# Forming the low half of unscaled weights by an accumulating DMA instead of a VectorE subtraction

## The chip, the cores and the metric

The kernel runs on one core of one Trainium2 chip. Its time is the device time of one execution, in microseconds. Engines are called TensorE (PE, and PEld for its weight loads), VectorE (DVE), ScalarE (ACT), GpSimd (POOL) and SyncE (SP, which issues most DMA transfers).

## The reference, cut to what matters

One layer of a hybrid decoder trunk on x of 1024 tokens by 1024 channels, in float32:

```python
shift, scale, gate = jnp.split(silu(c) @ ada_w + ada_b, 3, axis=-1)
h = rms_norm(x, norm_g) * (1 + scale) + shift
parts = jnp.split(h @ w_in, offsets, axis=-1)     # 16 column groups, 10264 columns
y_sb  = stick_breaking_attention(...) * silu(sz)  # 4 heads of 128
y_gdn = rms_norm(gated_delta_rule(...)) * silu(dz)
y_gla = rms_norm(gla_chunked(...)) * silu(lz)
g_sb, g_gdn, g_gla = jnp.split(sigmoid(mg + merge_b), 3, axis=-1)
merged = g_sb * (y_sb @ proj_sb) + g_gdn * (y_gdn @ proj_gdn) + g_gla * (y_gla @ proj_gla)
return x + gate * (merged @ w_out)
```

Most of the arithmetic is in the dense products: h with the columns of w_in, the three projections and w_out.

## The kernel before, in words

Everything is held transposed, channels on the 128 partitions. A dense product is made from two parts of each operand: the high part is the operand rounded to the fast float32r format, the low part is what the rounding left. Three passes of matmuls (high by high, low by high, high by low) go into one PSUM bank. `split` (L149 to L156) makes the two parts of a weight: ScalarE casts the raw tile into the high part (L151), VectorE subtracts the high part from the raw tile and writes the low part (L152). Where a row scale belongs to the weights, L154 and L155 do the same with the scale.

`load_half` (L161) brings four blocks of 128 rows by 128 columns, 256 KB, into a raw tile by a DMA on SyncE's queue (L163) and splits them. There are three raw tiles and three slots for finished weights (`w`, with both parts of up to eight blocks). `load_w` (L170) makes one slot from one or two halves, for a group of 128 output channels that `run_cm` (L187) works off with 24 matmuls per half of the tokens for eight blocks, or 12 for four. `load_tm` (L176) fills two slots, whi and wlo, for the products with tokens on the partitions; it calls `load_half` too.

`load_w` without a scale serves 56 groups of w_in (the delta rule's heads 1 to 3, the linear attention's q, k and two z for each of four heads, the attention's z, 24 merge gates), proj_sb (eight groups with four blocks) and w_out (eight groups). proj_gla and proj_gdn have scales. The four column groups of the first head of the delta rule advance together in a loop at the start, which calls `split` itself (L345).

Only TensorE's order is written by hand. A planner in the program (`emit`, L247) interleaves the tasks of the three mixers with the dense groups: each task yields estimated waits, and the dense groups fill the time between. `dense` (L234) asks for the weights of a group one group ahead. The order of the instructions on all other engines and on SyncE's queue is made by the framework's scheduler from its own estimates; each engine then runs its list in that order.

The stages: start, norm and the first head (0 to 84 us), the gates' inputs and the first conv (84 to 134 us), the gated delta rule beside dense groups (134 to 500 us), gated linear attention (to 860 us), stick-breaking attention (to 1181 us), merge and output (to 1522 us). In the delta rule each of eight half heads passes a list of small steps: `gdn_prep` (L500; a power on GpSimd in `rstd_cols`, L284; a round trip through DRAM, L555 to L560; 15 pairs of small VectorE steps, L570 and L572; xd out and in, L579 and L594), `gdn_inv` (L582; GpSimd's L596, L602, L628, L631), `gdn_vq` (L680; GpSimd's L720) and `gdn_scan` (L728). The gates' inputs pass GpSimd at L452 and L453, then ScalarE, a scan on VectorE (L473) and transposes on TensorE whose results VectorE copies at L489 and L490.

Of the kernel before, what the change touches and what calls it, by code (L numbers as in the profile page):

```python
# [12 lines left out]
F32 = mybir.dt.float32  # L13
F32R = mybir.dt.float32r
BF16 = mybir.dt.bfloat16
AF = mybir.ActivationFunctionType
ALU = mybir.AluOpType
AX = mybir.AxisListType

P = 128  # L20
# [32 lines left out]
def kernel(ctx: ExitStack, tc: tile.TileContext, xT: bass.AP, c: bass.AP,  # L53
# [3 lines left out]
    nc = tc.nc  # L57
# [15 lines left out]
    def big(tag, w=1024, dt=F32):  # L73
        return mp.tile([P, w], dt, tag=tag, name=tag, bufs=3 if tag == "u5" else 2)

    def mid(tag, w=512, dt=F32):
        return sp.tile([P, w], dt, tag=tag, name=tag, bufs=1 if tag in ONE_MID else 3 if tag in ("c0", "c8", "c9") else 2)
# [67 lines left out]
        mm(ps, ones[0:1, :], crow[0:1, sl], 858, start=True, stop=True)  # L145
        nc.scalar.activation(out=c_row[:, sl], in_=ps, func=AF.Silu)

# [1 line left out]
    def split(hi, lo, raw, scale=None):  # L149
        if scale is None:  # L150
            nc.scalar.copy(out=hi, in_=raw)  # L151
            nc.vector.tensor_sub(out=lo, in0=raw, in1=hi.bitcast(F32))  # L152
        else:
            nc.scalar.activation(out=hi, in_=raw, func=AF.Copy, scale=scale)  # L154
            nc.vector.scalar_tensor_tensor(out=lo, in0=raw, scalar=scale, in1=hi.bitcast(F32),  # L155
                                           op0=ALU.mult, op1=ALU.subtract)  # L156

    def raw_tile():
        return wp.tile([P, 4, P], F32, tag="raw", name="raw")

    def load_half(hi, lo, src, k0, scales=None):  # L161
        raw = raw_tile()
        nc.sync.dma_start(out=raw, in_=src[k0 * P:(k0 + 4) * P, :].rearrange("(k p) n -> p k n", p=P))  # L163
        if scales is None:
            split(hi, lo, raw)
        else:
            for k in range(4):
                split(hi[:, k, :], lo[:, k, :], raw[:, k, :], scales[k])

    def load_w(src, kt=KT, scales=None):  # L170
        w = wp.tile([P, 2, KT, P], F32R, tag="w", name="w")
        for k0 in range(0, kt, 4):
            load_half(w[:, 0, k0:k0 + 4, :], w[:, 1, k0:k0 + 4, :], src, k0, scales)
        return w

    def load_tm(offs):  # L176
        whi = wp.tile([P, KT, 2 * P], F32R, tag="w", name="whi")
        wlo = wp.tile([P, KT, 2 * P], F32R, tag="w", name="wlo")
        for i, o in enumerate(offs):
            cs = slice(i * P, (i + 1) * P)  # L180
            for k0 in (0, 4):
                load_half(whi[:, k0:k0 + 4, cs], wlo[:, k0:k0 + 4, cs], w_in[:, o:o + P], k0)
        return whi, wlo
# [38 lines left out]
            evac(t2, ps)  # L222
            yield

    # a dense group: (load, run); loads are issued one group ahead
    def cm_in(o, evac):
        return (lambda: load_w(w_in[:, o:o + P])), (lambda w: run_cm(w, evac()))

# [60 lines left out]
    def colb(ap, n, w):  # L289
        return ap.unsqueeze(2).broadcast_to([P, n, w])  # L290

# [1 line left out]
    mod = cp.tile([P, 24], F32, name="mod")  # L293

    def conditioning(j, t_w="u6", t_p="u3"):
# [27 lines left out]
    for hf in range(2):  # L323
        nc.scalar.activation(out=rstd[:, hf * HALF:(hf + 1) * HALF], in_=ms[hf], func=AF.Ln,
                             scale=1.0 / D, bias=eps_c)
    nc.scalar.activation(out=rstd, in_=rstd, func=AF.Exp, scale=-0.5)
    amp = cp.tile([P, KT], F32, name="amp")

    # the first head's four column groups advance together as h arrives
    first = (O_DQ, O_DK, O_DV, O_DZ)  # L330
    f_ps = [[None, None] for _ in first]
    f_banks = ((pa, "acc"), (pa, "acc"), (pm, "mx"), (pm, "mx"), (pt, "tr"), (pl, "lv"),
# [1 line left out]
    for k in range(KT):  # L334
        conditioning(k)
        conditioning(8 + k)
        raw = raw_tile()
        wsrc = w_in[k * P:(k + 1) * P, O_DQ:O_DQ + 4 * 512].rearrange("p (g n) -> p g n", g=4)
        nc.sync.dma_start(out=raw, in_=wsrc[:, :, 0:P])
        w = wp.tile([P, 2, 4, P], F32R, tag="w", name="w")  # L340
# [7 lines left out]
        hi = hp.tile([P, T], F32R, tag="h", name="h_hi")  # L348
        lo = hp.tile([P, T], F32R, tag="h", name="h_lo")
# [26 lines left out]
                    mm(f_ps[g][hf], w[:, a, g, :], r[:, sl], 216,  # L376
                       start=(k == 0 and n == 0), stop=(k == KT - 1 and n == 2))

# [1 line left out]
    def conv_silu(r, i, h):  # L380
        t = big(f"u{1 + i}")
        j = 4 * (4 * i + h)
        nc.vector.tensor_scalar(out=t, in0=r[:, 0:T], scalar1=C("conv", j), scalar2=None,
                                op0=ALU.mult)
        for tap in range(1, 4):
            nc.vector.scalar_tensor_tensor(out=t, in0=r[:, tap:tap + T],  # L386
                                           scalar=C("conv", j + tap), in1=t,
                                           op0=ALU.mult, op1=ALU.add)
        return t
# [35 lines left out]
        for hf in range(2):  # L425
            f(hf, slice(hf * HALF, (hf + 1) * HALF), f_ps[i][hf])

# [1 line left out]
    small_w = wp.tile([P, 2, KT, P], F32R, tag="w", name="w")  # L429
    nc.gpsimd.memset(small_w.rearrange("p a k n -> p (a k n)").bitcast(F32), 0.0)  # L430
    raw = big("u7").rearrange("p (k n) -> p k n", k=KT)
    for o, dst, n in ((O_LR, 0, RANK), (O_DB, 32, NH), (O_DA, 64, NH)):
        nc.sync.dma_start(out=raw[:, :, dst:dst + n],
                          in_=w_in[:, o:o + n].rearrange("(k p) n -> p k n", p=P))
# [5 lines left out]
    parts = [mid("v2", dt=F32R)[0:RANK, :] for _ in range(2)]  # L440
# [55 lines left out]
    g_dram = {e: dp.tile([P, T], F32, name=f"g_dram{e[0]}_{e[1]}") for e in EARLY}  # L496
    y_dram = [dp.tile([P, T], F32, name=f"y_dram{i}") for i in range(16)]

# [1 line left out]
    def gdn_prep(st, q):  # L500
        h = st["h"]
        hs = slice(q * HALF, (q + 1) * HALF)
# [290 lines left out]
                                    in0=o[:, i * width:(i + 1) * width],  # L793
                                    scalar1=rs[:, i:i + 1], scalar2=None, op0=ALU.mult)

# [1 line left out]
    def gla_groups(st):  # L797
        h = st["h"]

# [219 lines left out]
                                     in1=st["z"][e_][:, t0:t0 + 256])  # L1019
                nc.sync.dma_start(out=y_dram[8 + 2 * h + e_][:, t0:t0 + 256], in_=y)  # L1020

# [1 line left out]
    sb_v = {}  # L1023

    def sb_groups(st):
# [125 lines left out]
                nc.sync.dma_start(out=y_dram[h][:, sl], in_=y)  # L1151
            yield 1200

# [1 line left out]
    merged = []  # L1155
    gate_t = {}
    ys = {}
# [114 lines left out]
                    gs.append(gate(gi, d + 2))  # L1272
        return gs + [(out_group(d), []) for d in range(KT)]

# [1 line left out]
    L = [{"h": h, "z": []} for h in range(NH)]  # L1276
    SB = [{"h": h} for h in range(NH)]

# [105 lines left out]
```

## Time and profile before

| | |
|---|---|
| median of 3 runs | 1523.69 us (1520.3 to 1524.83) |
| profiled execution | span 1522.0 us, first to last instruction; no other time is shown for it |
| TensorE busy | 1463.0 us, 96% |
| weight loads (PEld) | 1227.5 us, 81% |
| VectorE busy | 861.8 us, 57% |
| ScalarE busy | 676.8 us, 44% |
| GpSimd busy | 175.8 us, 12% |
| DMA | 126.48 MB, mean 83 GB/s; SyncE's queue 27.9% of 16 engines |
| chain of waits | PE 81%, DVE 9%, ACT 4%, POOL 2%, issue 2%, DMA 2% |

A busy time is the sum of an engine's instructions; instructions that only issue a DMA or wait are not in it. The chain of waits is followed back from the last instruction: each piece is what released the next one. An arrow `<-` in a group reads "written from".

### The profile page before, as it was taken

Reading aid. Unit: us, or ns where it says so; the run is one execution under the profiler, and the core shown is the slowest. Engines: PE = TensorE matmul, PEld = TensorE weight load, DVE = VectorE, ACT = ScalarE, POOL = GpSimd, SP = SyncE. Lnnn points to the kernel's source line nnn. Section 1 sums busy time; section 2 is a strip of 40 time slices with the busy share of each in tenths; the row PEclk is TensorE's granted clock in tenths of the full one; section 3 lists DMA queues with packets and bytes.
Section 4 is the critical chain, followed back from the end, with each engine's and each line's share of the span. In section 5 each row is a group of like instructions: output and inputs, shape, how many; then the busy total and the mean of one; then the engine's idle time right before and its main releaser. Section 6 shows DMA issues by size and latency. Waiting matters only on the chain.

```text
span 1522.0 us, 26560 instructions
## 1 busy us (share of the span) xinstructions
PE 1463.0 (96%) x10564; PEld 1227.5 (81%) x10564; DVE 861.8 (57%) x1855; ACT 676.8 (44%) x1473; POOL 175.8 (12%) x306
## 2 busy tenths in 40 slices
PE   4898999999999999999999999999999999999998
PEld 1677787777778887978888999889988888888887
DVE  5978736557653666667666525563555226474621
ACT  4255845462652846556475524342444442322200
POOL 4231222223330000000000100000000000000000
PEclk8899999999999999999999999999999999999999
DMA  6644322131231211212121212111122334353342
GB/s 211 189 119 120 99 87 74 44 88 47 79 93 50 56 43 53 53 32 60 50 67 38 69 49 63 49 36 42 43 69 85 110 104 138 115 149 111 120 143 76
DMA packets 162470, 126.48 MB, mean 83 GB/s; under 512 B 23429, under 2 KB 139269, under 8 KB 162346
## 3 DMA queue, kind: packets, MB, share of 16 engines
q1 hardware_dynamic: 162202, 124.47, 27.9%
q8 instruction: 83, 1.36, 0.4%
q14 instruction: 41, 0.34, 0.1%
q10 hardware_dynamic: 144, 0.31, 0.1%
HBM read 99.80 MB, written 24.95 MB: 82 GB/s over the span
## 4 chain that ended last, share of the span: by engine, by line
PE 81%; DVE 9%; ACT 4%; POOL 2%; issue 2%; DMA 2%; SPq 0%; POOLq 0%; DVEq 0%; ACTq 0%
PE acc L95 66%; PE lv L95 6%; PE mx L95 6%; PE tr L122 3%; DVE u L299 1%; DVE w L152 1%; POOL c L284 1%; DVE u L386 1%; POOL u L453 1%; DVE w L570 1%; DVE w L572 1%; DVE u L1110 1%; DMA u<-in_adaT 1%; POOL w L596 0%; DMA w<-xd 0%
## 5 line engine op out<-in xcount | busy, mean ns | idle before, releaser
L95 PE MATMUL acc<-h_hi,w 128*128 128x512 f32 x1856 | 658.1, 409 | 12.4 <-ACT h_hi L151 5.7
L95 PEld LDWEIGHTS acc<-h_hi,w 128*128 128x128 f32 x1856 | 352.5, 190 | 84.5 <-ACT h_hi L151 6.1
L95 PE MATMUL acc<-h_lo,w 128*128 128x512 f32 x928 | 365.9, 394 | 8.1 <-DVE h_lo L358 7.7
L95 PEld LDWEIGHTS acc<-h_lo,w 128*128 128x128 f32 x928 | 176.9, 191 | 36.9 <-DVE h_lo L358 8.9
L95 PE MATMUL acc<-whi,h_hi 128*128 128x256 f32 x640 | 186.8, 292 | 0.0
L95 PE MATMUL acc<-whi,h_lo 128*128 128x256 f32 x640 | 180.7, 282 | 0.0
L95 PE MATMUL acc<-wlo,h_hi 128*128 128x256 f32 x640 | 180.7, 282 | 0.0
L95 PE MATMUL acc<-u,w 128*128 128x512 f32 x768 | 176.5, 391 | 0.0
L95 PEld LDWEIGHTS acc<-u,w 128*128 128x128 f32 x768 | 144.2, 188 | 31.6
L151 ACT CAST w<-raw 128x512 fp32r<-128x512 f32 x143 | 84.2, 619 | 121.8 <-PE acc L95 90.4
L152 DVE TENSOR_TENSOR w<-raw,w 128x512 fp32r<-128x512 f32 x143 | 98.5, 701 | 50.7 <-ACT w L151 49.9
L95 PEld LDWEIGHTS acc<-whi,h_hi 128*128 128x128 f32 x640 | 122.3, 191 | 1.4 <-issue 0.7
L95 PEld LDWEIGHTS acc<-wlo,h_hi 128*128 128x128 f32 x640 | 122.4, 191 | 0.1
L95 PEld LDWEIGHTS acc<-whi,h_lo 128*128 128x128 f32 x640 | 122.1, 191 | 0.0
L284 POOL TENSOR_TENSOR c<-c,mhalf 128x4 f32<-128x4 f32 (+1 forms) x56 | 54.7, 976 | 578.8 <-DVE c L282 577.4
L95 PE MATMUL acc<-m_hi,w 128*128 128x512 f32 x256 | 79.0, 389 | 0.0
L1110 DVE TENSOR_TENSOR_SCAN u<-u,zero_c 128x128 f32<-128x128 f32 (+7 forms) x32 | 43.4, 1356 | 36.1 <-ACT u L1108 36.1
L155 DVE SCALAR_TENSOR_TENSOR w<-raw,col,w 128x128 fp32r<-128x128 f32 x96 | 29.5, 349 | 55.3 <-ACT w L154 55.3
L95 PEld LDWEIGHTS mx<-r,u 128*128 128x128 f32 x288 | 44.1, 190 | 18.0 <-DVE r L751 4.9
L95 PEld LDWEIGHTS acc<-m_hi,w 128*128 128x128 f32 x256 | 48.0, 188 | 10.0
L95 PE MATMUL mx<-r,u 128*128 128x128 f32 x288 | 48.5, 281 | 6.3 <-POOL u L720 2.7
L95 PE MATMUL lv<-u,u 128*32 128x32 f32 (+5 forms) x528 | 49.2, 252 | 4.1 <-DVE u L653 4.1
(254 smaller groups left out, 2177.6 us busy)
## 6 DMA issues: line engine op xcount, KB each, us to landing
raw<-in_w_in SPq DMA_DIRECT2D x160, 256.0 KB, 3.0
u<-in_adaT SPq DMA_DIRECT2D x24, 512.0 KB, 3.5
g_dram<-v SPq DMA_DIRECT2D x36, 256.0 KB, 2.1
v<-g_dram SPq DMA_DIRECT2D x36, 256.0 KB, 2.6
u<-in_xT SPq DMA_DIRECT2D x16, 512.0 KB, 5.6
u<-y_dram SPq DMA_DIRECT2D x16, 512.0 KB, 3.8
v<-gam_d SPq DMA_DIRECT2D x16, 256.0 KB, 3.5
y_dram<-v SPq DMA_DIRECT2D x16, 256.0 KB, 2.0
```

The costliest lines, as they stand in the source:

```text
L95: return nc.tensor.matmul(out, lhsT=lhsT, rhs=rhs, **kw)
L122: nc.tensor.transpose(out=out, in_=in_, identity=ident[:k, :k])
L151: nc.scalar.copy(out=hi, in_=raw)
L152: nc.vector.tensor_sub(out=lo, in0=raw, in1=hi.bitcast(F32))
L155: nc.vector.scalar_tensor_tensor(out=lo, in0=raw, scalar=scale, in1=hi.bitcast(F32), op0=ALU.mult, op1=ALU.subtract)
L284: nc.gpsimd.tensor_tensor(out=out, in0=out, in1=mhalf[:, 0:n], op=ALU.pow)
L299: nc.vector.tensor_tensor_reduce(out=junk, in0=aw, in1=c_row, scale=1.0, scalar=0.0, op0=ALU.mult, op1=ALU.add, accum_out=mod[:, j:j + 1])
L386: nc.vector.scalar_tensor_tensor(out=t, in0=r[:, tap:tap + T], scalar=C("conv", j + tap), in1=t, op0=ALU.mult, op1=ALU.add)
L453: nc.gpsimd.tensor_scalar(out=gt[0][DA, sl], in0=raw[DA, :], scalar1=C("dt_bias")[DA, :], scalar2=None, op0=ALU.add)
L570: nc.vector.tensor_tensor(out=t3, in0=L3[:, w:16, j:w].broadcast_to([32, n, w]), in1=Xl3[:, j:w, 0:w].broadcast_to([32, n, w]), op=ALU.mult)
L572: nc.vector.tensor_sub(out=Xl3[:, w:16, 0:w], in0=Xl3[:, w:16, 0:w], in1=t3)
L1110: nc.vector.tensor_tensor_scan(om[:, 0:n][:, ::-1], om[:, 0:n][:, ::-1], zero_c.broadcast_to([P, n]), 1.0, ALU.mult, ALU.add)
```

## The change

`load_half` gets a flag that only `load_w` sets. For an unscaled load whose source and destination both have 128 columns, ScalarE casts the raw tile into the high part as before, then writes the negated high part into the low part's place with a second activation, and GpSimd issues a DMA that adds the raw tile (SBUF) onto it (SBUF), each partition's 512 elements as one run. `split` is as it was and still serves the scaled weights, `load_tm`, the first head's loop and all activations. The rest of the diff removes or empties comment lines.

```diff
-    def load_half(hi, lo, src, k0, scales=None):
+    def load_half(hi, lo, src, k0, scales=None, by_dma=False):
         raw = raw_tile()
         nc.sync.dma_start(out=raw, in_=src[k0 * P:(k0 + 4) * P, :].rearrange("(k p) n -> p k n", p=P))
-        if scales is None:
+        if scales is None and hi.shape[-1] == P and src.shape[-1] == P and by_dma:
+            def flat(t):
+                return t.rearrange("p k n -> p (k n)")
+
+            nc.scalar.copy(out=hi, in_=raw)
+            nc.scalar.activation(out=lo, in_=hi.bitcast(F32), func=AF.Copy, scale=-1.0)
+            nc.gpsimd.dma_start(out=flat(lo), in_=flat(raw), accum_op=ALU.add)
+        elif scales is None:
             split(hi, lo, raw)
         else:
             for k in range(4):
...
         for k0 in range(0, kt, 4):
-            load_half(w[:, 0, k0:k0 + 4, :], w[:, 1, k0:k0 + 4, :], src, k0, scales)
+            load_half(w[:, 0, k0:k0 + 4, :], w[:, 1, k0:k0 + 4, :], src, k0, scales, True)
         return w
```

## Rows read from the trace of the kernel before

**Rows 1.** The page's head: span, busy us (share) xinstructions of each engine.

```profile
span 1522.0 us, 26560 instructions
...
PE 1463.0 (96%) x10564; PEld 1227.5 (81%) x10564; DVE 861.8 (57%) x1855; ACT 676.8 (44%) x1473; POOL 175.8 (12%) x306
```

**Rows 2.** Stages by window: us, busy us of each engine, granted clock, DMA share, GB/s.

```profile
core 0: us, PE busy (x) PEld busy (x) DVE busy (x) ACT busy (x) POOL busy (x), PEclk, DMA share, GB/s
84.00:134.00 50.00, 43.52 (x191) 35.23 (x190) 39.02 (x61) 31.65 (x43) 12.48 (x8) 0.96 0.38 107
134.00:500.00 366.00, 350.87 (x2826) 282.58 (x2826) 213.56 (x646) 190.83 (x469) 98.33 (x197) 0.98 0.28 76
500.00:860.00 360.00, 358.63 (x3689) 304.21 (x3688) 235.38 (x545) 217.10 (x404) 17.54 (x41) 1.00 0.20 54
860.00:1181.00 321.00, 317.10 (x2204) 290.07 (x2203) 158.64 (x248) 119.09 (x339) 17.81 (x30) 1.00 0.18 53
1181.00:1522.00 341.00, 337.06 (x1481) 277.27 (x1479) 150.18 (x260) 88.86 (x177) 0.00 (x0) 1.00 0.39 118
```

**Rows 3.** The chain of waits from 134 to 500 us, shares by line.

```profile
by line: PE acc L95 49.6%; PE lv L95 7.9%; PE mx L95 7.1%; issue 3.7%; POOL c L284 2.8%; DVE w L570 2.7%; DVE w L572 2.5%; PE tr L122 2.2%; POOL w L596 1.9%; DMA w<-xd 1.9%; ACT v L530 1.2%; DVE w L152 1.2%; DVE u L386 1.1%; PE lv L122 1.1%
```

**Rows 4.** The page's costliest groups: xcount, busy us, mean ns, idle before.

```profile
L151 ACT CAST w<-raw 128x512 fp32r<-128x512 f32 x143 | 84.2, 619 | 121.8 <-PE acc L95 90.4
L152 DVE TENSOR_TENSOR w<-raw,w 128x512 fp32r<-128x512 f32 x143 | 98.5, 701 | 50.7 <-ACT w L151 49.9
```

**Rows 5.** The chain from 84 to 134 us: start us, us, what.

```profile
100.84 8.96 POOL u L453
...
116.37 0.62 ACT w L151
...
129.42 0.60 DVE w L152
```

**Rows 6.** Instructions in order of time, 98 to 133 us: start, us, instruction, idle before.

```profile
103.54 0.67 DVE L152 TENSOR_TENSOR w<-raw,w 128x512 fp32r<-128x512 f32 x1
...
105.34 1.27 DVE L152 TENSOR_TENSOR w<-raw,w 128x512 fp32r<-128x512 f32 x2
...
110.71 1.56 POOL L453 TENSOR_SCALAR u<-v,col 4x512 f32<-4x512 f32 x1
...
132.40 1.09 PE L122 MATMUL tr<-cst,u 128*128 128x128 f32 x4 [4.68 <-DVE gam_c L490]
```

**Rows 7.** The chain from 140 to 250 us, first and last of three.

```profile
171.35 0.51 ACT w L151
...
242.17 0.52 ACT w L151
```

**Rows 8.** Windows of 10 us, columns as in group 2.

```profile
130.00:140.00 10.00, 7.60 (x27) 6.34 (x28) 9.94 (x24) 6.88 (x11) 0.10 (x1) 0.67 0.75 214
...
320.00:330.00 10.00, 9.18 (x54) 7.66 (x53) 7.88 (x29) 9.20 (x26) 4.02 (x7) 1.00 0.49 136
```

**Rows 9.** GpSimd's groups, L284 of 134 to 500 us.

```profile
L284 POOL TENSOR_TENSOR c<-c,mhalf 128x4 f32<-128x4 f32 x23 | 24.9, 1083 | 61.3 <-DVE c L282 61.1
...
L783 POOL MEMSET c<- 128x4 f32 x24 | 2.4, 100 | 0.1
```

**Rows 10.** DMA issues: xcount, KB each, median us to landing.

```profile
raw<-in_w_in SPq DMA_DIRECT2D x160, 256.0 KB, 3.0
...
y_dram<-v SPq DMA_DIRECT2D x16, 256.0 KB, 2.0
```

**Rows 11.** Instructions in order of time, 1380 to 1440 us.

```profile
1386.85 44.13 PE L95 MATMUL acc<-u,w 128*128 128x512 f32 x192
...
1392.56 0.62 ACT L151 CAST w<-raw 128x512 fp32r<-128x512 f32 x1 [4.31 <-PE acc L95]
...
1393.21 0.69 DVE L152 TENSOR_TENSOR w<-raw,w 128x512 fp32r<-128x512 f32 x1
```

**Rows 12.** SyncE's queue from 134 to 500 us: us waited, times, longest.

```profile
SPq L163 <- DVE w L152: 69.4, 22, 10.2
```

## The prediction

> **What bounds the kernel now.** I read the busy shares first. TensorE is busy 1463.0 of a span of 1522.0 us, VectorE 57%, ScalarE 44%, GpSimd 12% [rows 1]: the reader is to see one engine that is nearly always at work, so that only its idle time, and the clock that it loses after idling, can be given back. Second, the stages [rows 2]. From 134 to 500 us TensorE is idle 366.0 - 350.9 = 15.1 us and its granted clock is 0.98 of the full 2.4 GHz, which is worth 0.02 x 366 = 7.3 us more. From 84 to 134 us it is idle 6.5 us at 0.96 (2.0 us). The three later stages together have 9.2 us of idle at full clock, and the last of them sits mostly behind the last matmul. So the change can only gain between 84 and 500 us, where the gated delta rule runs beside the dense groups. Third, the chain of waits in that stage [rows 3]: TensorE holds most of it, but VectorE's L570, L572 and L152, GpSimd's L284 and L596 and a transfer have a per cent or two each. The edited lines are on the chain, though thinly.
>
> **What it removes.** The loads with no scale are 12 + 16 + 4 + 24 = 56 groups of w_in with two halves, 8 of proj_sb with one and 8 of w_out with two: 136 subtractions, the 143 of the group [rows 4] less the 7 of the first head's loop, which calls split itself. At 701 ns that is 95 us of VectorE. What counts is what of it lies on the chain. Between 134 and 500 us L152 has 1.2% of 366 us = 4.4 us [rows 3]. Before that, the chain goes through an instruction of GpSimd: L453 took 8.96 us [rows 5], and its twin 1.56 us [rows 6]. In those 8.96 us VectorE ran three of the subtractions (0.67 + 1.27 = 1.94 us) among other work without a pause [rows 6], so GpSimd was held back for as long as VectorE was busy. I count the 1.9 us; the bounds are 0 (other work moves up and holds it as long) and 7.4 us (it runs like its twin). One more piece of 0.60 us is on the chain at 129.42 [rows 5], ahead of the copy for which TensorE waits 4.68 us at 132.40 [rows 6]. Together 4.4 + 1.9 + 0.6 = 6.9 us.
>
> **What it adds on ScalarE.** A second pass over each tile of 128x512: the nearest row is the cast of the same shape, 619 ns [rows 4], so 136 x 0.62 = 84 us, ScalarE going from 677 to 761 us of 1522. Most of it lies in time in which ScalarE is free. Where the cast itself is on the chain a second pass comes on top: three such pieces from 171.35 to 242.17 us, 1.6 us [rows 7], and one of 0.62 at 116.37 [rows 5], 2.2 us in all. Below that it can be 0 (the scheduler moves the passes). Above, ScalarE is already busy 9.20 of 10 us where a half head starts [rows 8]: two passes in each of the eight such places, nothing hidden, are 8 x 2 x 0.62 = 9.9 us. I take 2.2, the rows that are on the chain.
>
> **What it adds on GpSimd.** It issues 136 transfers where it issued none. What an issue takes no row shows. The nearest are its small instructions: 0.10 us for a memset and 1.08 us for L284 on 128x4 [rows 9]; the far end is 5.26 us, the mean of the two L453. I take 1.08, as an instruction whose few elements don't explain its time. The 44 loads from 134 to 500 us then hold GpSimd 48 us, 13% of the stage. On the chain GpSimd has L284 with 2.8% and L596 with 1.9% [rows 3], 17.2 us, or some 19 pieces of 0.9 us. Each meets an issue with 13% and waits half of it: 19 x 0.13 x 0.54 = 1.3 us. At 0.10 us it is nothing; at 5.26 us the share is 63% and 19 x 0.63 x 2.63 = 32 us. Three issues fall where L453 stands, up to 3.2 us; I take one, 1.1 us. An issue also waits in GpSimd's queue for ScalarE's second pass, with the small powers of L284 behind it; this is in the upper end, not in the sum.
>
> Here the trace shows VectorE holding GpSimd up: 8.96 against 1.56 us [rows 5, 6]. The Trainium skill (SBUF — State Buffer, section "SBUF: two separate sides") says that the two share a port pair that is locked for a whole instruction, and that a GpSimd that is locked out cannot write the descriptors of its own transfers, so that such a DMA looks blocked by VectorE. [...]
>
> **The transfer, and when the low part is there.** A transfer of 256 KB lands in 2.0 us (y_dram<-v) to 3.0 us (raw<-in_w_in) [rows 10]; this one also reads what it adds to, so the ends are 2.0 and twice 3.0. I take 3.0. The low part then comes 0.62 + 1.08 + 3.0 - 0.70 = 4.0 us later than now. The tightest place is proj_sb: 192 matmuls in 44.13 us are eight groups of 5.5 us [rows 11]. The cast at 1392.56 fills the slot of the first group and is for the fourth, which starts at 1386.85 + 3 x 5.5 = 1403.4; the subtraction is done at 1393.9 [rows 11]. The slack is 9.5 us, the other groups are longer: TensorE doesn't wait for weights, cost 0. If that cover were gone, each microsecond beyond it would be paid up to eight times here.
>
> The raw tile is held the same 4.0 us longer, and SyncE, which issues in order, already waits for L152 to let go of one 22 times from 134 to 500 us, 69.4 us in all [rows 12]. Behind it stand the round trips of the delta rule and the stores. If each of the 22 holds the queue 4.0 us longer, that is 88 of 366 us, 24%; w<-xd has 1.9% of the chain [rows 3], 7.0 us, some 4 or 5 pieces, each then with 0.24 x 2.0 us: 2.4 us. The lower end is 0, where the scheduler puts the others ahead. I take the middle, 1.2 us.
>
> **The sum.** -6.9 + 2.2 + 1.3 + 1.1 + 1.2 = -1.1 us of idle. A microsecond of idle in this stage costs half of one more in clock (7.3 to 15.1), so -1.6 us. The profiled execution is known by its span alone, 1522.0 us; the median of the runs, 1523.69, lies 1.7 us above it, which I take for what lies around the span. 1522.0 - 1.6 + 1.7 = 1522.1 us.
>
> **The rivals.** (a) VectorE was what held the delta rule's steps, and the additions all find cover: the whole 6.9 us comes back, with the clock 6.9 x 1.5 = 10.3, and the time is 1513.3 us. For it: L570 and L572 wait on VectorE in order, and the slice 130 to 140 us has VectorE at 9.94 of 10 with TensorE at a clock of 0.67 [rows 8]. Against: ScalarE is as full in places, and the lines of the change are 1.2% of the chain.
>
> (b) Slower, by GpSimd's queue: its issues are held up by VectorE, as L453 was, and L284 and L596 stand behind them. With 3.2 us an issue (between 1.08 and 5.26) the share is 44 x 3.2 / 366 = 38%, and 19 x 0.38 x 1.6 = 11.6 us in place of 1.3, so -1.1 + 10.3 = 9.2, x 1.5 = 13.8: 1537.5 us. It decides from about 1.5 us an issue, where 19 x 0.18 x 0.75 = 2.6 eats the gain left without that term (2.4). For it: L453. Against: GpSimd is idle most of the stage, 98 us busy of 366 [rows 2].
>
> (c) Slower, by ScalarE: the 9.9 us in place of 2.2: 6.6 x 1.5 = 9.9, 1533.6 us. For it the slice with 9.20 of 10; against, that half of the stage's ScalarE time is free.
>
> (d) The transfer is far slower than a plain one, say 12 us later than the subtraction: 2.5 us beyond the slack, eight times, 20 us: 1543.7 us. Nothing in the trace speaks for it but that no row shows such a transfer.
>
> That the change doesn't reach the loads is no case: the slices end in 128 columns on both sides for every unscaled load of load_w.
>
> **How the numbers follow.** The forecast, no change that can be told, has 0.37 (1517 to 1527), (a) 0.33, (b) 0.16, (c) 0.09, (d) 0.05. About 0.3% (4.6 us) is what a measurement of this kernel tells from no change. Faster is (a) and the lower edge of the forecast, 0.34; slower (b), (c), (d), less their mild forms, 0.28; the same 0.38. The range leaves out part of (d), the worse half of (b) and the largest gains (L453 at its twin's time): 1510 to 1538.
>
> **What would show it.** Right: VectorE's busy time falls by about 95 us, ScalarE's rises by about 84, 136 transfers of 256 KB appear on GpSimd, TensorE's idle from 134 to 500 us stays within some 5 us of 15.1, and no weight load waits for a transfer. L453 should be shorter than 8.96 us. Wrong: L284 or L596 with longer waits and an issue ahead of them (b), ScalarE's activations behind second passes on the chain (c), weight loads waiting for DMA (d), or idle under 9 us in that stage (a).

## The result: slower by 1.4%, and the profile after

The kernel with the change takes 1541.99 us (median of 4 runs, 1541.09 to 1548.45); the kernel before, on the same chip, takes 1523.69 (1520.3 to 1524.83 in three executions; a fourth took 5582.91 us and is left out). The ratio is 1.0137 (95% interval 1.0113 to 1.0162); the two medians alone give 1.0120. The forecast was 1522.1 us, no change that can be told, with a range from 1510 to 1538; the time is 4 us above its upper end. The profiled execution has a span of 1539.3 us against 1522.0, so 17.3 us are to be found. TensorE's idle time has 10.0 of them; its busy time, for the same 10564 matmuls, is 7.3 us longer.

First the busy shares and the stages of the kernel after, as in [rows 1, 2] (all lines behind `load_half` are 7 higher than before).

```profile
span 1539.3 us, 26927 instructions
...
PE 1470.3 (96%) x10564; PEld 1229.5 (80%) x10564; DVE 783.9 (51%) x1719; ACT 750.0 (49%) x1610; POOL 289.0 (19%) x442
```

```profile
core 0: us, PE busy (x) PEld busy (x) DVE busy (x) ACT busy (x) POOL busy (x), PEclk, DMA share, GB/s
84.00:134.00 50.00, 44.45 (x188) 35.18 (x187) 34.42 (x55) 36.13 (x51) 17.76 (x17) 0.97 0.68 168
134.00:500.00 366.00, 345.83 (x2803) 279.00 (x2802) 185.39 (x595) 211.05 (x509) 132.65 (x241) 0.98 0.46 104
500.00:860.00 360.00, 354.10 (x3608) 295.27 (x3607) 215.90 (x509) 228.05 (x417) 40.27 (x66) 1.00 0.31 72
860.00:1181.00 321.00, 316.25 (x2224) 290.78 (x2223) 144.42 (x228) 130.67 (x371) 36.63 (x52) 1.00 0.28 70
1181.00:1539.30 358.30, 351.44 (x1555) 289.05 (x1553) 135.88 (x235) 113.35 (x221) 31.20 (x36) 0.99 0.54 142
```

VectorE has 78 us less to do, ScalarE 73 and GpSimd 113 more (an issue on GpSimd does count as busy time, unlike one on SyncE: the 136 issues are 120.5 us of GpSimd's 289.0). TensorE's idle time grows by 5.0 us between 134 and 500 us (20.2 against 15.1), but also by 4.5 us between 500 and 860 us (5.9 against 1.4), a stage from which the prediction expected nothing. Fixed windows slide against the work, so the loss is better dated by events. These are six points of TensorE's work, which has the same order in every version: the starts of the fourth group of transposes (L122; 147.12 us before), the first product of each linear-attention head's v group (heads 1 and 4: 523.13 and 789.64), the first such group of the attention (847.43), the first output product (1430.81), and the end (1522.0). The table gives each kernel's delay against the kernel before; the experiments' edits follow below. Each row of delays is one profiled execution. Over 15 executions the time of the kernel before alone went from 1517.53 to 1525.27 us, so a delay of 2 or 3 us at the start can be chance; the points from head 1 on agree within 0.1 us where an edit does nothing there (e9, e10).

| kernel | transposes | head 1 | head 4 | attention | output | end | ratio of the times (95%) |
|---|---|---|---|---|---|---|---|
| after | -2.9 | +2.8 | +10.1 | +11.3 | +12.2 | +17.3 | 1.0137 (1.0113 to 1.0162) |
| e1_dram | -5.3 | -0.2 | +2.0 | +3.1 | +2.2 | +2.4 | 1.0044 (1.0026 to 1.0062) |
| e2_hold | -0.5 | +5.4 | +5.4 | +6.5 | +6.4 | +6.6 | 1.0058 (1.0040 to 1.0076) |
| e3_actpass | -1.2 | 0.0 | +2.2 | +3.2 | +5.4 | +5.4 | 1.0032 (1.0014 to 1.0049) |
| e4_noout | -2.7 | +4.3 | +11.3 | +12.6 | +16.9 | +17.5 | 1.0143 (1.0117 to 1.0168) |
| e5_dveneg | +3.2 | +7.3 | +7.8 | +7.9 | +14.2 | +15.6 | 1.0131 (1.0105 to 1.0157) |
| e6_after_raw4 | -2.5 | +6.5 | +13.3 | +14.8 | +26.8 | +27.6 | 1.0190 (1.0166 to 1.0214) |
| e7_before_raw4 | -1.4 | +7.6 | +20.2 | +24.8 | +35.3 | +35.3 | 1.0261 (1.0237 to 1.0285) |
| e9_poolonly | -2.7 | -0.8 | -0.7 | -0.7 | -0.7 | -0.7 | 1.0030 (1.0015 to 1.0044) |
| e10_store | +0.6 | +1.6 | +1.6 | +1.6 | +1.6 | +1.8 | 1.0031 (1.0022 to 1.0040) |
| e12_dram_dveneg | -2.8 | +6.8 | +6.9 | +7.1 | +6.5 | +6.7 | 1.0050 (1.0035 to 1.0065) |
| e13_dram_holdraw | -0.9 | +10.2 | +12.3 | +14.3 | +13.5 | +13.6 | 1.0104 (1.0089 to 1.0119) |
| e14_dram_holdhi | -2.9 | +5.0 | +7.2 | +8.2 | +8.3 | +8.5 | 1.0073 (1.0053 to 1.0092) |
| e15_dram_longraw | +3.8 | +41.0 | +48.1 | +51.0 | +77.3 | +81.1 | 1.0592 (1.0559 to 1.0624) |
| e16_dram_longhi | +0.6 | +33.2 | +40.4 | +41.5 | +44.3 | +44.4 | 1.0323 (1.0306 to 1.0340) |

In the kernel after, the start gains 2.9 us, the delta rule (to head 1) loses 5.7, the three linear-attention heads from head 1 to head 4 lose 7.4 (about 2.5 each), the next two stretches 1.2 and 0.9, and the output stage 5.1: 17.3 in all. Now its costliest groups, as in [rows 4, 9, 10] (count, busy us, mean ns, idle before), and the row of the transfer (its last column is the median time from issue to landing):

```profile
L170 POOL DMA_DIRECT2D w<-raw x136 | 120.5, 956 | 709.4 <-ACT w L169 651.0
L168 ACT CAST w<-raw 128x512 fp32r<-128x512 f32 x136 | 80.7, 618 | 134.6 <-PE acc L95 97.6
L291 POOL TENSOR_TENSOR c<-c,mhalf 128x4 f32<-128x4 f32 (+1 forms) x56 | 57.1, 1020 | 276.5 <-DVE c L289 269.9
```

```profile
w<-raw POOLq DMA_DIRECT2D x136, 256.0 KB, 3.9
```

An issue takes GpSimd 0.956 us and the transfer lands in 3.9 us: what was priced at 1.08 and 3.0. So no single new operation is dear. The next view, SyncE's waits between 134 and 500 us (total us, times, longest), answers to [rows 12], where the same queue waited 69.4 us, 22 times, for the subtraction:

```profile
SPq L163 <- DMA w<-raw: 144.7, 40, 13.0
```

The raw tile is now let go by the accumulating transfer, not by VectorE. What that does is seen in a linear-attention head. These rows are in order of time (start, us, instruction, in brackets the idle time before it and what ended it):

```profile
551.83 0.62 ACT L168 CAST w<-raw 128x512 fp32r<-128x512 f32 x1 [4.90 <-PE acc L95]
...
552.83 0.63 ACT L169 ACTIVATE w<-w 128x512 fp32r<-128x512 f32 x1
...
553.76 0.86 POOL L170 DMA_DIRECT2D w<-raw  x1 [18.67 <-ACT w L169]
...
557.10 5.76 SPq L163 DMA_DIRECT2D raw<-in_w_in  x3
...
560.30 0.48 DVE L1002 SCALAR_TENSOR_TENSOR r<-r,c,mx 128x256 f32<-128x256 f32 x1 [1.53 <-PE mx L95]
...
563.09 0.62 ACT L168 CAST w<-raw 128x512 fp32r<-128x512 f32 x1 [6.35 <-DMA raw<-in_w_in]
563.62 0.59 ACT L283 ACTIVATE u<-acc 128x512 f32<-128x512 f32 x1
564.10 0.62 ACT L169 ACTIVATE w<-w 128x512 fp32r<-128x512 f32 x1
564.62 0.39 ACT L151 CAST w<-r 128x256 fp32r<-128x256 f32 x1
...
565.07 0.96 PE L95 MATMUL mx<-w,u 128*128 128x256 f32 x3 [1.09 <-ACT w L151]
```

Read it as a loop. The cast starts at 551.83; the second pass, GpSimd's issue and the landing hold the raw tile until 557.10, 5.3 us, where cast and subtraction took about 1.3 (0.62 + 0.70 by [rows 4]). (Pairing casts and releases in order of time, the median hold of all loads is about 6.5 us, 1.4 before.) Only then does SyncE refill it (L163, the first of the three in that row). The refill is there at 563.09, 6.0 us later, where the median of these loads is 3.1; ScalarE, which works through its list in order, has then stood 6.35 us before a cast whose product is far off. Behind that cast stands a small cast (w<-r, L151) for which TensorE waits. VectorE had written its input by 560.78 (L1002), and it starts at 564.62. The weights are not late; the engine that makes them is, for other work. In the output stage the same loop shows on the chain of waits (start us, us, what):

```profile
1434.17 5.67 DMA w<-raw
...
1439.94 4.14 DMA raw<-in_w_out
...
1444.10 0.62 ACT w L168
1444.72 0.96 ACT m_hi L151
...
1451.25 83.98 PE acc L95 x362
```

A landing of 5.67 us, a refill of 4.14, a cast, and then the split of the merged channels (m_hi), for which TensorE waits. Before the change no transfer stood on the chain there. TensorE stands 2.0 us for m_hi and 0.8 us for m_lo, and in the slice that follows its granted clock is 0.58, mostly the lower of its two levels, 1.2 and 2.4 GHz (columns as in the stages above):

```profile
1452.00:1456.00 4.00, 4.00 (x12) 3.12 (x12) 0.75 (x1) 0.00 (x0) 0.00 (x0) 0.58 0.78 145
```

Of the 5.1 us lost in the output stage 2.9 are idle time and 2.2 longer busy time. These are ScalarE's waits for a raw tile of `load_w` from 500 to 870 us, after and before; in the output stage the longest has 5.1 us after, and before there is none:

```profile
ACT w L168 <- DMA raw<-in_w_in: 16.7, 3, 6.3
```

```profile
ACT w L151 <- DMA raw<-in_w_in: 7.5, 3, 3.4
```

### The profile page after: what moved, and what is told of

The parts are those of the page before. It is cut to its first block, busy times and chain, and to the rows that moved or that the text cites. A ratio compares the mean times of both kernels' runs of the same rounds, so it can differ in the third digit from the quotient of the medians.

```text
span 1539.3 us, 26927 instructions
## 1 busy us (share of the span) xinstructions
PE 1470.3 (96%) x10564; PEld 1229.5 (80%) x10564; DVE 783.9 (51%) x1719; ACT 750.0 (49%) x1610; POOL 289.0 (19%) x442
## 3 DMA queue, kind: packets, MB, share of 16 engines
q1 hardware_dynamic: 162202, 124.47, 27.8%
## 4 chain that ended last, share of the span: by engine, by line
PE 67%; ACT 5%; DVE 4%; DMA 4%; issue 3%; POOL 1%; SPq 0%; DVEq 0%; POOLq 0%; ACTq 0%
PE acc L95 56%; PE mx L95 5%; PE lv L95 4%; PE tr L122 2%; DMA w<-raw 2%; DMA raw<-in_w_in 1%; POOL c L291 1%; ACT L864 1%; ACT w L168 1%; DVE w L579 0%; DVE w L577 0%; DMA v<-gam_d 0%; ACT w L169 0%; DVE u L1117 0%; DVE u L870 0%
## 5 line engine op out<-in xcount | busy, mean ns | idle before, releaser
L170 POOL DMA_DIRECT2D w<-raw x136 | 120.5, 956 | 709.4 <-ACT w L169 651.0
L168 ACT CAST w<-raw 128x512 fp32r<-128x512 f32 x136 | 80.7, 618 | 134.6 <-PE acc L95 97.6
L291 POOL TENSOR_TENSOR c<-c,mhalf 128x4 f32<-128x4 f32 (+1 forms) x56 | 57.1, 1020 | 276.5 <-DVE c L289 269.9
L169 ACT ACTIVATE w<-w 128x512 fp32r<-128x512 f32 x136 | 82.6, 628 | 0.9
L1117 DVE TENSOR_TENSOR_SCAN u<-u,zero_c 128x128 f32<-128x128 f32 (+7 forms) x32 | 43.4, 1356 | 41.5 <-ACT u L1115 41.4
```

Of the source, the lines that this page charges most:

```text
L169: nc.scalar.activation(out=lo, in_=hi.bitcast(F32), func=AF.Copy, scale=-1.0)
L170: nc.gpsimd.dma_start(out=flat(lo), in_=flat(raw), accum_op=ALU.add)
L291: nc.gpsimd.tensor_tensor(out=out, in0=out, in1=mhalf[:, 0:n], op=ALU.pow)
L1117: nc.vector.tensor_tensor_scan(om[:, 0:n][:, ::-1], om[:, 0:n][:, ::-1], zero_c.broadcast_to([P, n]), 1.0, ALU.mult, ALU.add)
```

## The experiments

The theory is that loop: the raw tile's hold, and ScalarE's in-order wait for the refill. The rivals are ScalarE's second pass, GpSimd's issues (its queue), and the extra transfers as such.

**e1_dram: the accumulating transfer reads the weights from memory a second time**, so the raw tile is free after the cast.

```diff
-            nc.gpsimd.dma_start(out=flat(lo), in_=flat(raw), accum_op=ALU.add)
+            nc.gpsimd.dma_start(out=lo, in_=src[k0 * P:(k0 + 4) * P, :].rearrange("(k p) n -> p k n", p=P),
+                                accum_op=ALU.add)
```

> The accumulating transfer reads the weights from HBM instead of the raw tile; the second ScalarE pass, the GpSimd issue and the later low part stay. Theory raw (the raw tile is held until the accumulating transfer lands, so its refill comes late, SyncE stands in front of other transfers and ScalarE's next cast blocks the work behind it): the raw tile is free after the cast, the 17 us go away, 1519 to 1527 us. Rival ScalarE (the second passes are what is late): nothing changes, 1538 to 1546. Rival GpSimd (the issues are): the same or slower, 1540 to 1550, since an issue of 512-byte pieces costs more.

Measured: 1527.61 us, ratio 1.0044 (1.0026 to 1.0062); 14.9 of the 17.3 us of span are gone (by the ratios 0.93 of 1.37 per cent). Every instruction of ScalarE is still there, and on GpSimd each issue is dearer and each landing later than in the kernel after (group and transfer, as above):

```profile
L170 POOL DMA_DIRECT2D w<-in_w_in x112 | 147.6, 1492 | 550.7 <-ACT w L169 542.3
```

```profile
w<-in_w_in POOLq DMA_DIRECT2D x112, 256.0 KB, 5.8
```

An issue of 1.49 us for 0.96 and a landing of 5.8 us for 3.9 would make it slower, if issue or transfer were the price. It is faster, and what else differs is when the raw tile goes free. SyncE's waits for it over the whole run, in e1, in the kernel after and in the kernel before:

```profile
SPq L163 <- ACT w L168: 370.0, 81, 23.7
```

```profile
SPq L163 <- DMA w<-raw: 529.4, 123, 23.3
```

```profile
SPq L163 <- DVE w L152: 303.7, 88, 23.2
```

In e1 ScalarE has no wait left for a raw tile of `load_w` from 500 to 870 us, and in the output stage the chain holds TensorE alone again:

```profile
1424.94 95.34 PE acc L95 x420
```

The 14.9 us are 3.0 up to head 1, 5.2 in the heads, 1.9 up to the output and 4.9 in it.

**e2_hold: VectorE's subtraction kept, a plain store of the raw tile added on GpSimd.**

```diff
+            hold = dp.tile([P, 4 * P], F32, tag="hold", name="hold", bufs=8)
+            nc.gpsimd.dma_start(out=hold, in_=flat(raw))
```

> The kernel before with its VectorE subtraction, and beside it, for the same 136 loads, a plain transfer of the raw tile to unused DRAM issued by GpSimd: it holds the raw tile and issues on GpSimd, without the second ScalarE pass and without a late low part. Theory raw: slower than before by most of the 17 us, and by some 3 us more since VectorE gets no relief, 1536 to 1545. Rival ScalarE: like before, 1521 to 1528. Rival late low part (TensorE waits for the low parts themselves): like before too. Rival GpSimd: slower as in theory raw; the place tells them apart, since after 1181 us GpSimd has nothing else to do, and theory raw wants about 5 us there.

Measured: 1529.53 us, ratio 1.0058, under the range of the theory (1536 to 1545) and a little above that of the rivals (to 1528). The store starts as soon as the raw tile is there, beside the cast, so it was seldom what let the tile go: SyncE's refills waited for it 25.3 us in all, against 529.4 for the accumulating transfer. As an experiment on a long hold it is weak. It shows that issue and traffic cost nothing from head 1 to head 4 and nothing in the output stage; 5.9 of its 6.6 us are lost in the delta rule and 1.1 in head 4.

**e3_actpass: ScalarE's second pass alone**; VectorE adds the raw tile, and there is no transfer.

```diff
-            nc.gpsimd.dma_start(out=flat(lo), in_=flat(raw), accum_op=ALU.add)
+            nc.vector.tensor_tensor(out=lo, in0=raw, in1=lo.bitcast(F32), op=ALU.add)
```

> The second ScalarE pass alone: ScalarE writes the negated high part into the low part's place, and VectorE adds the raw tile onto it; no transfer, no GpSimd. Theory raw: the raw tile is held 0.6 us longer, so at most a few us, 1522 to 1529. Rival ScalarE: the whole slowdown or more, 1536 to 1545.

Measured: 1525.82 us, ratio 1.0032, in the range of the theory (1522 to 1529). The profiled execution took 1529.21 us, the longest of seven. In it the delta rule loses 1.2 us, three of the four linear-attention heads 1.1 each and the stretch before the output 2.2. TensorE's waits between 500 and 860 us name it: the first row below is there in e1 and in the kernel after too (2.4 us, 3 times), and it is missing in the kernel before and in e12 further down, which have no second pass on ScalarE.

```profile
PE tr L122 <- DVE v L945: 2.5, 3, 0.8
PE mx L95 <- DVE w L152: 1.1, 3, 0.4
```

**e4_noout: the change without proj_sb and w_out**, which go back to the subtraction.

```diff
-        return (lambda: load_w(proj[row0:row0 + 512, d * P:(d + 1) * P], 4, scales)), run
+        return (lambda: load_w(proj[row0:row0 + 512, d * P:(d + 1) * P], 4, scales, False)), run
...
-            w = load_w(w_out[:, d * P:(d + 1) * P])
+            w = load_w(w_out[:, d * P:(d + 1) * P], by_dma=False)
```

> The change without the loads of proj_sb and w_out, which go back to the VectorE subtraction. Theory raw, and any in which the place of the loss is the step from proj_sb to w_out: about 5 us less than the changed kernel, 1535 to 1539 us, with the last stage as long as before (some 341 us from the first projection). A theory in which the loss is spread over all loads: 1 to 2 us less, 1540.

Measured: 1542.31 us, ratio 1.0143, no better than the change itself; the 1535 to 1539 us of the theory were missed. The output stage is back (0.6 us lost for 5.1), but 4.3 us are lost before it for 0.9. There the chain has an accumulating transfer (3.64 us) and the refill behind it (2.89) of a load that kept the change; that these are the whole loss is not shown. A part that is taken back locally is lost again ahead of it, so the per-stage sums don't simply add.

**e5_dveneg: the negation on VectorE**, the raw tile held as in the change.

```diff
-            nc.scalar.activation(out=lo, in_=hi.bitcast(F32), func=AF.Copy, scale=-1.0)
+            nc.vector.tensor_scalar(out=lo, in0=hi.bitcast(F32), scalar1=-1.0, scalar2=None, op0=ALU.mult)
```

> The change with the negation on VectorE in place of ScalarE: no second ScalarE pass, but the raw tile is held as long as in the changed kernel. Theory raw alone: the stage from 500 to 860 us and the step from proj_sb to w_out lose as much as in the changed kernel (8 and 5 us), 1538 to 1543 us in all. Theory both (a long hold puts ScalarE's casts late, and the second passes lengthen the pile behind them): the 500 to 860 us stage loses some 5 of its 8 us, the last stage still about 5, 1533 to 1538 us. Rival ScalarE: both go, 1524 to 1530 us.

Measured: 1539.47 us, ratio 1.0131. The time is in the range of the hold alone (1538 to 1543), the places are not. The heads lose 0.5 us in all in place of 7.4, the output stage 1.4 in place of 5.1, but the stretch between attention and output loses 6.3 in place of 0.9 and the start 3.2, where the change gained 2.9. ScalarE still waits 13.7 us, 3 times, for raw tiles of `load_w` from 500 to 870 us: what such a wait costs depends on the work behind it. So in heads and output the loss needs both, the hold and ScalarE's second pass (which also lengthens the hold), and the hold without the second pass costs about as much in all, elsewhere.

**e6_after_raw4 and e7_before_raw4: a fourth raw tile**, on the kernel after and the one before. To make room three pairs of other tiles become single.

```diff
-    ONE_MID = ("w0", "w2", "w3", "w4", "w5", "w7", "v5")
+    ONE_MID = ("w0", "w2", "w3", "w4", "w5", "w7", "v5", "w6", "r0", "r1")
...
-        return wp.tile([P, 4, P], F32, tag="raw", name="raw")
+        return wp.tile([P, 4, P], F32, tag="raw", name="raw", bufs=4)
```

> The changed kernel with four raw tiles in place of three; the room comes from three small tags of the delta rule (w6, r0, r1) with one buffer in place of two. To be read against the kernel before with the same edit. Theory raw: the step to w_out and the stage from 500 to 860 us lose at most half of what they lose in the changed kernel, so 6 to 10 us between the two, where the changed kernel has 17 to the kernel before. Rivals ScalarE and GpSimd: 15 to 20 us between the two, as without the fourth tile.

> The kernel before with four raw tiles and the same three tags at one buffer, the control. If the single buffers cost the delta rule a wait, it is slower than the kernel before, by 0 to 10 us; a fourth raw tile alone should give it nothing, since nothing in it waits for weights after 500 us.

Measured: 1549.12 and 1559.94 us. The single tiles cost far more than the raw tile could give (+35.3 us on the kernel before), which spoils the comparison with the kernels of three raw tiles. Between the two the order is turned round: with four raw tiles the change is 10.8 us faster than the subtraction. And the output stage loses 0.8 us for 5.1. Both fit the theory; neither is clean.

**e9_poolonly: the kernel before with a GpSimd operation per load**, a power on 128x4 elements, 1.28 us in the mean, nothing else.

```diff
             split(hi, lo, raw)
+            if by_dma:
+                nc.gpsimd.tensor_tensor(out=cp.tile([P, 4], F32, tag="jk", name="jk"), in0=hi[:, 0, 0:4].bitcast(F32), in1=mhalf[:, 0:4], op=ALU.pow)
...
```

> The kernel before with a power on 128x4 on GpSimd for each of the 136 loads, which waits for the cast and takes about 1.0 us, as long as an issue; no transfer, no second pass, nothing reads its result. Theory GpSimd queue (the 5 us that every kernel with issues on GpSimd loses between 150 and 520 us come from GpSimd's queue): 4 to 6 us slower, all of it before 520 us. Rival traffic (they come from the transfers, which slow the delta rule's round trips, or from SyncE's queue): within 2 us of the kernel before.

Measured: 1525.44 us, ratio 1.0030, with a profiled span of 1521.3. More GpSimd time than the issues take (0.96 us each) costs 0.3% by the times and nothing by the profiled execution, which was the shortest of ten (1523.06 us), so where the 0.3% lie is not shown; in it no stage loses from head 1 on. It has the start's gain of 2.7 us too, with all subtractions in place.

**e10_store: as e2, but the store reads the high part.**

```diff
-            nc.gpsimd.dma_start(out=hold, in_=flat(raw))
+            nc.gpsimd.dma_start(out=hold, in_=flat(hi).bitcast(F32))
```

> The kernel before, with its VectorE subtraction and one ScalarE pass, and a plain store of the high part (256 KB) issued on GpSimd per load: traffic and issue without the raw tile's hold and without a second ScalarE pass. Theory (the loss between 134 and 500 us is transfers and issues): that stage loses as in e2 (5.9 us between the first transposes and the first linear-attention head), time 1527 to 1530. Rival (it is the raw tile's hold): under 2 us there, 1522 to 1525.

Measured: 1526.08 us, ratio 1.0031 (1.0022 to 1.0040). The delta rule loses 1.0 us, not 5.9: the first reading falls for this stage, though the time lies a little above the rival's. 136 issues and 35 MB of traffic without a hold cost 0.3% by the times and 1.8 us in the profiled execution.

**e12_dram_dveneg: e1 with the negation on VectorE** (0.43 us a pass, 0.70 for the subtraction).

```diff
-            nc.scalar.activation(out=lo, in_=hi.bitcast(F32), func=AF.Copy, scale=-1.0)
+            nc.vector.tensor_scalar(out=lo, in0=hi.bitcast(F32), scalar1=-1.0, scalar2=None, op0=ALU.mult)
```

> e1 with the negation on VectorE (one operand) in place of ScalarE: no raw hold, no second ScalarE pass, VectorE's subtraction replaced by a cheaper pass. Theory (what e1 still loses, about 1 us per linear-attention head, is the second ScalarE pass): the four heads lose under 0.5 us each, 1521 to 1525. Rival (the late low part or the extra transfer costs that): heads lose about 1 us each as in e1, 1526 to 1529.

Measured: 1529.03 us, ratio 1.0050. The heads lose 0.1 us in all: what e1 loses there is the second ScalarE pass, and the row of TensorE's waits shown under e3 is gone. The time was missed, since the delta rule loses 9.6 us; there GpSimd's issues wait for VectorE (466.0 of their 612.0 us of idle time).

**e13_dram_holdraw and e14_dram_holdhi: e1 with a plain store behind the accumulating transfer**, of the raw tile or of the high part.

```diff
+            hold = dp.tile([P, 4 * P], F32, tag="hold", name="hold", bufs=8)
+            nc.gpsimd.dma_start(out=hold, in_=flat(raw))
```

```diff
+            nc.gpsimd.dma_start(out=hold, in_=flat(hi).bitcast(F32))
```

> The weights are read a second time from memory by the accumulating transfer (as in e1), and GpSimd issues behind it a plain store of the raw tile to a scratch tensor, which nothing reads. So the raw tile is held again until a GpSimd transfer lands, behind two issues. Theory (the raw tile's hold, together with the second ScalarE pass, delays the refill): the loss of the change comes back, some 8 to 18 us over e1's 1527.6, 1536 to 1546, with GLA heads losing 2 us each and the output stage some 5. Rival (second transfers and issues cost by themselves): the same as e14, whatever that is.

> The twin of e13: same issues, same bytes, but the plain store reads the high part (which stays anyway until the products are done) and not the raw tile. Theory (raw hold): near e1, 1527 to 1531, at least 6 us under e13, with no transfer of raw on the output stage's chain. Rival (traffic and issues): equal to e13 within 2 us.

Measured: 1537.56 and 1532.69 us. Same bytes, same issues, 4.9 us apart (5.1 of span), all of it by head 1. The sizes were missed: e14 has a ratio of 1.0073 where e1 has 1.0044, some 4 us, so traffic and issues have a price of their own on top of e1, and e13 loses nothing more in heads and output. The store had been put ahead of waiting accumulations in GpSimd's list, so it held the raw tile 88.5 us of SyncE's time in all, not the 529.4 of the change.

**e15_dram_longraw and e16_dram_longhi: the long hold by itself.** e1, and per load a GpSimd addition on 128x4 elements that waits for the landed low part and reads the raw tile in the one, the high part in the other.

```diff
+            nc.gpsimd.tensor_tensor(out=cp.tile([P, 4], F32, tag="jk", name="jk"), in0=raw[:, 3, P - 4:],
+                                    in1=lo[:, 3, P - 4:].bitcast(F32), op=ALU.add)
```

```diff
+            nc.gpsimd.tensor_tensor(out=cp.tile([P, 4], F32, tag="jk", name="jk"), in0=hi[:, 3, P - 4:].bitcast(F32),
+                                    in1=lo[:, 3, P - 4:].bitcast(F32), op=ALU.add)
```

> e1 (the accumulating transfer reads the weights from memory) and, per load, a GpSimd addition on 128x4 of the raw tile and the finished low part, whose result nothing uses. It holds the raw tile until the low part has landed, as the change does, by one small read; GpSimd waits in order for each landing. Theory (long hold with the second ScalarE pass makes the loss in the linear-attention heads and in the output stage): beyond its twin e16 it loses some 1.5 us more in each of the four heads and some 5 us more at the start of the output products, 10 us or more in all, and the raw transfer stands on the output stage's chain. Rival (what e1 took away was something else, the source in SBUF for one): equal to e16 within 2 us.

> The twin of e15: the same GpSimd addition waits for the same landing, but reads the high part and not the raw tile, so the raw tile is free after the cast. Theory: it may lose in the delta rule, where GpSimd's other work stands behind the waits, but in the linear-attention heads it loses only e1's 1 us each and in the output stage under 1 us. Rival (source in SBUF): equal to e15.

Measured: 1614.5 and 1570.77 us, ratios 1.0592 (1.0559 to 1.0624) and 1.0323 (1.0306 to 1.0340). They differ in the tile that a read of 128x4 elements holds, and by 43.7 us. In SyncE's waits (whole run) and on the chain of the output stage the first has

```profile
SPq L163 <- POOL jk L172: 480.2, 118, 9.3
```

```profile
1501.07 7.69 DMA w<-in_w_out x2
...
1510.10 2.94 DMA raw<-in_w_out
...
1513.15 0.63 ACT w L168
1513.80 0.63 ACT w L169
1514.43 0.94 ACT m_hi L151
```

and the second, whose chain there is TensorE alone,

```profile
SPq L163 <- ACT w L168: 378.4, 80, 23.7
```

```profile
1399.86 162.49 PE acc L95 x714
```

That is the loop of the change, made and unmade by one operand. Its size is not that of the change: the tile is held longer (a median of about 8.6 us), and between attention and output TensorE also waits 2.7 us, in 2 waits, for late low parts of proj_sb, which it never does in the change. The places were partly missed: of the 36.7 us of span the pair differs by 7.8 at head 1, 1.8 in head 4, 23.5 between attention and output and 3.7 in the output stage (5 expected), but the heads are equal (7.1 and 7.2 from head 1 to head 4), so for them the hold is shown by e1 and by the rows, not by this pair. That e16 itself is 44 us slower is GpSimd standing 305 us in wait for landings (231.8 + 44.1 + 29.5 by its idle times) with the delta rule's work behind; the change has no such wait.

No version beats the kernel before: the best by span, e9, does more work and has a ratio of 1.0030. By the ratios the versions fall into groups. Where the accumulating transfer reads the raw tile (the change, e4, e5) they are 1.0131 to 1.0143; where none does and at most one is added (e1, e3, e9, e10, e12) 1.0030 to 1.0050. With two transfers a load e14 has 1.0073 without a hold and e13 1.0104 with a partial one; e16, where GpSimd waits for landings, is beside this row. So the hold is the larger part of the change's loss, wherever it falls.

## Why the prediction was wrong

**The step that failed** is the raw tile's longer hold. The prediction had it: 4.0 us longer, 22 refills, SyncE's queue held 88 us more. The hold was nearly right (5.3 us for 1.3 in the case shown, about 5.1 us more in the median), and so was the queue (75 us more in that stage: 144.7 for 69.4). The price was not. It was put at 1.2 us, between 0 and 2.4, for the delta rule's round trips behind SyncE alone. Freeing the raw tile gives back 14.9 us of span (e1). What was left out is the other side of the refill: it comes later, and ScalarE, which takes its list in order, stands before the cast with work behind it that is due now. The sentence "TensorE doesn't wait for weights, cost 0" checked when TensorE needs the low part, 9.5 us of slack at proj_sb, and that slack held: among TensorE's waits in the kernel after there is none for an accumulating transfer. The tile that decides is the source, not the destination: three raw tiles make a closed loop of load, cast, release and load, and lengthening one leg lengthens the loop wherever it was nearly full. The row of [rows 12] hinted that it was: SyncE waited for a raw tile in 22 places of one stage. The prediction read that row for its queue and not for its loop. So it also looked for costs in the delta rule only, while 12 of the 14.9 us lie after head 1. Its sign of being right, an idle time within some 5 us of 15.1 from 134 to 500 us, was met (20.2) beside a wrong time.

**The factor of 1.5 for the clock** came near: 17.3 us of span go with 10.0 of idle. But the rest is not all clock. From head 1 to head 4 TensorE's busy time grows by 3.6 us at a granted clock of 1.00 in both kernels; what makes it longer is not shown.

**VectorE's relief, -6.9 us**, was not found as a gain. The long L453 is shorter, as foreseen (after L460, GpSimd, in order of time, against 8.96 and 1.56 in [rows 5, 6]):

```profile
98.91 6.03 POOL L460 TENSOR_SCALAR u<-v,col 4x512 f32<-4x512 f32 x1
...
106.78 1.57 POOL L460 TENSOR_SCALAR u<-v,col 4x512 f32<-4x512 f32 x1
```

That is 2.9 us for 1.9 expected, and the start is 2.9 us early. But e9 is as early with every subtraction in place and its L453 at 8.95, so the start's gain is not shown to be VectorE's relief; another order of the same lists gives as much. It is lost again by head 1. Where VectorE keeps a pass (e5 against after, e12 against e1), head 1 comes 4.6 and 7.0 us later, which is the size of the term; but in these GpSimd's issues wait for VectorE as well, so this is a hint and no proof.

**VectorE's and ScalarE's busy time**: 78 us less and 73 more, for 95 and 84. The pass on ScalarE takes 0.63 us, as priced; instructions back to back overlap (two subtractions in 1.27 us, [rows 6], where one takes 0.70), and mean times 136 counts the overlap twice.

**ScalarE's second pass, +2.2 us**, was low and in the wrong place: e3 costs 4.0 us by the medians and 5.4 in its profiled execution, where 3.2 are in the linear attention, 2.2 ahead of the output, and the 1.2 of the delta rule are no more than the start gains.

**GpSimd's issues, +1.3 and +1.1 us**, were right in size (0.956 us each). The waits of VectorE for the powers of L291 in the delta rule grew from 22.3 us (9.1 + 6.8 + 6.4) to 27.8 (10.1 + 9.4 + 8.3). The Trainium skill (SBUF — State Buffer, section "SBUF: two separate sides") says that GpSimd cannot write the descriptors of its transfers while VectorE runs an operation in a 2-port performance mode; it does not say so of every operation. Here the 136 issues have a median of 0.87 us and a longest of 1.55, so this trace shows no issue held up as L453 was.

**The rivals.** (b) and (c) had the right sign and not the mechanism: GpSimd's work alone (e9) and ScalarE's pass alone (e3) give 1525.4 and 1525.8. (d) came out nearest in time, 1543.7, with "weights late" as its reason; the transfer is not slow (3.9 us), and TensorE does not wait for weights. The right number there would have been an accident.

**What stays open.** In the delta rule stage every edit moves head 1 against the transposes, by 1 to 11 us (33 and 37 in e16 and e15), even a store for which SyncE waits only 13 times (e2, 5.9 us, where e10 loses 1.0). The instruction lists are ordered anew for every edit. The change loses 5.7 us there and e1, without the hold, 5.1, so how much of it is the hold and how much the new order is not settled. Nor is the loss by the hold in the heads separated from the second pass beyond e1 and e5: both are needed. Why e5 loses 6.3 us between attention and output, where the change loses 0.9, is not shown.

## What to carry to other kernels

When a step is moved to a DMA, ask what each of its operands holds until it lands, the source first: with a few rotating tiles the landing goes into the loop of load, use, release and reload, and the next load's user pays, on whatever engine waits for it in order. A queue that already waits for buffers at many places is the row to price this from, once for the queue and once for each in-order engine that uses the refilled tile. If such a transfer is wanted, let it read a source that nobody waits for (e1: 14.9 of 17.3 us back, with a slower transfer).

## What the runs showed that was not expected

An accumulating transfer of 256 KB from SBUF onto SBUF lands in 3.9 us (median), against 3.0 us for the plain load [rows 10], and takes GpSimd 0.96 us to issue where each partition's 2 KB is one run. From memory, in runs of 512 bytes, issue and landing are 1.49 and 5.8 us. Beside a second GpSimd transfer of the same size (e14) the landing from memory grows to 6.7 us.
